# Seven-product feed-forward blocks: row sums on VectorE, kept gate blocks, gate products first, another order of banks

## The chip, the cores and the metric

The kernel runs on one NeuronCore of a Trainium2 chip. The metric is the device time of one execution in microseconds (us). Engines are named as in the profile: PE is TensorE (PEld its weight loads), DVE is VectorE, ACT is ScalarE, POOL is GpSimd, and SP is SyncE, which here does nothing but issue DMAs.

## The reference

The program is a two-layer streaming encoder on 256 rows of 1024 channels, all in float32:

```
h += 0.5 * ffn(rmsnorm(h)); h += mixer(rmsnorm(h)); h += 0.5 * ffn(rmsnorm(h))     # per layer
ffn(x) = (silu(x @ w1) * (x @ w3)) @ w2        # 1024 -> 2816 -> 1024
```

The mixer of layer 0 is a convolution module, that of layer 1 is latent attention, and a last rmsnorm ends it. So there are four feed-forward blocks (FFNs), counted 0 to 3 here as in the code. Their weights are most of what is read from HBM and their products most of the work on PE.

## The kernel before, in words

**Split weights and rows.** A float32 product is made of three passes of a faster matmul type: every weight block and every row block is kept as a high part and a low part. `mm3` (L325) issues the three matmuls high x low, high x high and low x high. A weight block is 128 x 2048 floats, 1 MB. `load` (L215 to L245) fetches it with one DMA on SP's queue into one of four `raw` buffers. Then, in two halves of 1024 columns, ACT casts the high part (L241) and DVE subtracts it from the block to get the low part (L242); `hi` and `lo` have five buffers each. The DMAs of a block are issued when one of the four raw buffers has been read for the last time.

**An FFN.** `ffn_in` (L807) runs the up products in chunks `c` = 0 to 5 of 512 gate columns (256 in the last). Chunk by chunk, two row tiles `tb` and two matrices (m = 0 for w1, m = 1 for w3) fill four PSUM banks `u[m, tb]`. ACT then takes the silu of `u[0, tb]` (L914), DVE multiplies it with `u[1, tb]` (L915), and `turn` (L810) brings the gate block into transposed form: DVE transposes 32 x 32 blocks (L445), four DMAs write the tile to DRAM, one reads it back in another order into the tile `gb` (L449, L453), and ACT and DVE split it into `Gh` and `Gl` (L816, L817). The down product (class `Rows`, L719) then sums over the 22 gate blocks into four banks `o[tb, d]`.

**Seven products in place of eight.** In FFNs 1, 2 and 3, chunk 3 of the up product and the first eight gate blocks of the down product are computed as a 2 x 2 block product with seven block products (`seven_products`, L348). One block product is 12 matmuls. The seven need sums and differences of blocks on both sides:

- of the weights: `load_seven` (L190 to L211) makes them on DVE in the raw buffers with four subtractions of 128 x 2048, at L201 and L202 (before the second block), L204 (before the third) and L206 (before the seventh). The high and low parts of all seven come at L210;
- of the rows: `forms_of` (L333) adds high and low parts on POOL (L339), makes four sums or differences of 128 x 512 on POOL (L343), and ACT and DVE split each (L344, L345). It works in the tile `rows4`. For the up product it is called ahead of chunk 2, for the down product after chunk 5. The split sums lie in gate columns that are not in use yet, or in the place of the FFN's own rows X once those have been read.

Between the products, results are copied or added from bank to bank, by the queue of each engine in order: after product 1, ACT copies bank `c11` to `c21`; after product 2, ACT copies `c22` to SBUF (`kept`); after product 3, DVE makes `c12 = c21 + kept`; after product 5, DVE makes `c22 = c21 + kept` (all L253 in the profile, since they are called through `urgent`). Product 2 is the first to write bank `c22`. Product 5 writes `c21` again, so it waits for the addition after product 3.

**What sets the order.** The code is traced in program order, and a planner decides at build time in which order each engine's instructions stand, from due order and an own timeline. `urgent` (L247) gives the instructions traced in it a higher priority, and remembers the last of them on each engine. `behind` (L182) adds to an instruction an edge that keeps it after the last six remembered ones of its engine; `load` calls it for the casts and low parts of ordinary blocks (L244), `load_seven` does not. `weights` (L266) hands out the next block, and `load_ahead` traces loads three blocks beyond it. So when the seven products begin, the loads of their blocks 0 to 2 have been traced ahead of the gate products (L915) of the chunk before, and blocks 3, 4, 5 and 6 are traced in products 1, 2, 3 and 4.

**Banks.** `bank("A", ...)` hands out four PSUM banks in turn; a new tile can be written when the last reader of the one before in its bank is done. The banks of the seven products were those of the chunk before, whose last readers are the gate products of L915.

Of the kernel before, what the change touches and what calls it, by code (L numbers as in the profile page):

```python
# [11 lines left out]
F32 = mybir.dt.float32  # L12
F32R = mybir.dt.float32r
# [27 lines left out]
W_BUFS = 5  # L41
# [48 lines left out]
def trunk(ctx: ExitStack, tc: tile.TileContext, x, xt, first, pos, invf, gfin, wdw,  # L90
          f1w13, f1w2, f2w13, f2w2, cw1, cw2, wa, wuq, wukv, wo, wpair, out):
    nc = tc.nc
# [12 lines left out]
    def uid(s):  # L105
        n_uid[0] += 1
        return f"{s}_{n_uid[0]}"
# [4 lines left out]
    def bank(tag, name):  # L112
        return ps.tile([P, 512], F32, tag=tag, name=uid(name), bufs=BANKS[tag])
# [75 lines left out]
    def load_seven(j, four, b, pieces):  # L189
        hi = wp.tile([P, HB], F32R, tag="hi", name=uid("hi"))  # L190
        lo = wp.tile([P, HB], F32R, tag="lo", name=uid("lo"))
        n = len(loaded)
        if j == 0:
            b[11], b[12] = fetched(four[0]), fetched(four[1])
        elif j == 1:
            b[22] = fetched(four[3])
        elif j == 2:
            b[21] = fetched(four[2])
        sub = nc.vector.tensor_sub
        if j == 1:  # L200
            sub(b[11], b[12], b[11])  # L201
            sub(b[12], b[22], b[12])  # L202
        elif j == 2:
            sub(b[11], b[22], b[11])  # L204
        elif j == 6:
            sub(b[11], b[21], b[11])  # L206
        raw = b[(11, 11, 11, 21, 12, 22, 11)[j]]
        for i in range(pieces):
            c = slice(i * HB // pieces, (i + 1) * HB // pieces)
            casts[n, i] = nc.scalar.copy(hi[:, c], raw[:, c]), sub(lo[:, c], raw[:, c], hi[:, c].bitcast(F32))  # L210
        return hi, lo  # L211

    def load(src, pieces=1):
# [46 lines left out]
    def load_ahead(ahead=W_BUFS - 2):  # L260
        load_to(min(len(blocks), n_used[0] + ahead))
# [5 lines left out]
    def weights(n=1, more=True):  # L267
        out = []
        for _ in range(n):
            n_used[0] += 1  # L270
            if more:
                load_ahead()
            else:
                load_ahead(0)
            out.append(loaded[n_used[0] - 1])
        return out
# [53 lines left out]
        nc.tensor.matmul(o, ah, bh, start=False, stop=False, skip_group_check=seeded)  # L330
        return nc.tensor.matmul(o, al, bh, start=False, stop=stop, skip_group_check=seeded)  # L331

    def forms_of(xh, xl, sh, sl):  # L333


        sh, sl = (z.rearrange("p k t -> p (k t)").rearrange("p (n k t) -> p n k t", n=4, t=P) for z in (sh, sl))
        x = rows4.rearrange("p n t -> p (n t)").rearrange("p (k t) -> p k t", t=S)
        add = nc.gpsimd.tensor_tensor
        add(x, xh.bitcast(F32), xl.bitcast(F32), op=ALU.add)  # L339
        x11, x12, x21, x22 = (x[:, 4 * a:4 * a + 4, tbs(tb)] for tb in range(2) for a in range(2))  # L340
        for n, out, left, right, op in ((0, x22, x21, x22, ALU.add), (2, x21, x11, x21, ALU.subtract),
                                        (1, x11, x22, x11, ALU.subtract), (3, x12, x12, x11, ALU.subtract)):
            add(out, left, right, op=op)  # L343
            nc.scalar.copy(sh[:, n], out)  # L344
            nc.vector.tensor_sub(sl[:, n], out, sh[:, n].bitcast(F32))  # L345
        return [(sh[:, n], sl[:, n]) for n in range(4)]
# [35 lines left out]
    def tbs(tb):  # L382
        return slice(tb * P, (tb + 1) * P)
# [53 lines left out]
                order(low, a.ins)  # L437
        return high

    def turn_blocks(pool, src, n, tag, after=()):  # L440
# [11 lines left out]
        b = pool.tile([P, 512], F32, tag=tag + "b", name=uid(tag + "b"), bufs=2)  # L452
        last_read[0] = nc.sync.dma_start(b[:, :w], d)  # L453
        return b[:, :w].rearrange("p (i t q) -> p t i q", i=4, q=32)

    class Norm:


        def __init__(self, gname, half=False, turn_by_dma=None):
            self.col = GCOL[gname]  # L460
            self.half = half

            self.pool = turn_by_dma
            self.turning = []
# [12 lines left out]
            self.turned = ()  # L477
            self.lows, self.highs = [], []

            self.between = None  # L480
# [236 lines left out]


    class Rows:  # L719
        def __init__(self, zh, zl, nk, last=False):  # L720
            self.zh, self.zl, self.nk, self.last = zh, zl, nk, last
            self.o = {(tb, d): bank("A", "o") for tb in range(NT) for d in range(2)}
            self.seeded = False

        def seven(self, forms):
            self.seeded = True
# [80 lines left out]
    def ffn_in(act, X, make_next, beside, apart, seven_up, seven_down):  # L807
        Gh = act.tile([P, NF, S], F32R, tag="Gh", name=uid("Gh"))
        Gl = act.tile([P, NF, S], F32R, tag="Gl", name=uid("Gl"))
        def turn(c, tb, w, g):  # L810

            n = w // P
            f = slice(4 * c, 4 * c + n)
            bv = turn_blocks(act, g[:, :w], n, "g")
            gh = Gh[:, f, tbs(tb)].rearrange("p t (i q) -> p t i q", q=32)
            nc.scalar.copy(gh, bv)  # L816
            nc.vector.tensor_sub(Gl[:, f, tbs(tb)].rearrange("p t (i q) -> p t i q", q=32), bv, gh.bitcast(F32))  # L817
# [30 lines left out]
        for c in range(6):  # L848

            both = c == 5  # L850
# [61 lines left out]
            for tb in range(NT):  # L912
                s = tmp.tile([P, 512], F32, tag="s", name=uid("s"))
                nc.scalar.activation(s[:, :w], u[0, tb][:, :w], AF.Silu, scale=X.r[tb])  # L914
                nc.vector.tensor_mul(s[:, :w], s[:, :w], u[0, tb][:, w:] if both else u[1, tb])  # L915
                turn(c, tb, w, s)
        o = Rows(Gh, Gl, NF, make_next is Final)
# [849 lines left out]
```

## Time and profile before

| | |
|---|---|
| median of 3 runs | 961.84 us (960.57 to 962.07) |
| the profiled execution: its own time | 960.39 us |
| its span, first to last instruction | 958.4 us |
| mean granted TensorE clock | 0.977 |
| PE busy | 902.6 us (94%), 4233 matmuls |
| DVE busy | 750.2 us (78%) |
| ACT busy | 546.6 us (57%) |
| POOL busy | 215.0 us (22%) |
| HBM | 207 GB/s over the span |

FFN 1 runs from about 278 us of the span, FFN 2 from about 470 us and FFN 3 from about 759 us. Rows of the profile name a line, an engine, an operation, the tiles written and read (out<-in), a shape and a count; then come busy time and the mean ns of one, or start and duration. In square brackets or at the end stands the idle time of the engine just ahead and what ended it. In the view by windows the columns are, for each stretch, the busy time and the count of PE, PEld, DVE, ACT and POOL, then the granted TensorE clock, the DMA engines' busy share and GB/s. `x2` behind a DVE row of L210 or L242 means two halves of a block.

### The profile page before, as it was taken

The numbers are of one execution on the slowest core, as the hardware profiler recorded it, in microseconds if no ns is written. First come the engines' busy times: TensorE is split into PE (matmuls) and PEld (weight loads), VectorE is DVE, ScalarE is ACT, GpSimd is POOL, SyncE is SP. The second block draws the span as 40 slices with busy tenths as digits, with TensorE's granted clock in tenths as the row PEclk, the third lists the DMA queues.
The fourth block names the chain that finished last, engine by engine and source line by source line (L and its number), as shares of the span: only waits on it lengthen the run. The fifth ranks groups of instructions, "written<-read, shape, count | busy, mean of one in ns | idle before, by whom it ended". The sixth has DMA issues, their size and how long they took to land.

```text
span 958.4 us, 12212 instructions
## 1 busy us (share of the span) xinstructions
PE 902.6 (94%) x4233; PEld 754.3 (79%) x4233; DVE 750.2 (78%) x1036; ACT 546.6 (57%) x917; POOL 215.0 (22%) x289
## 2 busy tenths in 40 slices
PE   9999999999999969989999499799999999599797
PEld 7888888898988858868888388688998888378686
DVE  5896654499988899895697989965866698988953
ACT  7655443598966346474463553753866663463742
POOL 1720000199925060000150600002300150600000
PEclk9999999999999989999999889999999999899999
DMA  9987775344138809578568086685635367095631
GB/s 332 361 318 264 244 245 198 132 176 151 70 84 317 297 20 364 179 249 301 160 218 283 9 311 224 195 312 155 220 122 207 124 234 279 3 343 192 207 156 44
DMA packets 71054, 198.94 MB, mean 208 GB/s; under 512 B 12368, under 2 KB 41936, under 8 KB 51664
## 3 DMA queue, kind: packets, MB, share of 16 engines
q1 hardware_dynamic: 70560, 197.47, 58.7%
q10 hardware_dynamic: 432, 0.69, 0.2%
q8 instruction: 33, 0.54, 0.2%
q14 instruction: 29, 0.24, 0.1%
HBM read 181.87 MB, written 16.25 MB: 207 GB/s over the span
## 4 chain that ended last, share of the span: by engine, by line
PE 46%; DVE 27%; DMA 14%; issue 7%; ACT 3%; SPq 2%; DVEq 0%; ACTq 0%
PE o L327 8%; PE o L331 8%; PE o L330 8%; DVE lo L210 7%; DVE lo L242 6%; DMA gb<-gd 4%; DMA raw<-in_f2w 4%; PE u L330 3%; PE u L327 3%; PE u L331 3%; DMA gd<-gt 3%; DVE acc L1045 2%; DVE raw L204 2%; PE u L956 2%; PE gate L956 2%
## 5 line engine op out<-in xcount | busy, mean ns | idle before, releaser
L242 DVE TENSOR_TENSOR lo<-raw,hi 128x1024 fp32r<-128x1024 f32 (+1 forms) x244 | 309.1, 1309 | 77.8 <-ACT hi L241 77.4
L241 ACT CAST hi<-raw 128x1024 fp32r<-128x1024 f32 (+1 forms) x246 | 244.2, 1044 | 130.0 <-PE o L331 54.3
L327 PE MATMUL u<-lo,Xh 128*128 128x512 f32 x612 | 238.4, 389 | 0.1
L330 PE MATMUL u<-hi,Xh 128*128 128x512 f32 x612 | 238.1, 389 | 0.0
L331 PE MATMUL u<-hi,Xl 128*128 128x512 f32 x612 | 237.7, 389 | 0.0
L327 PEld LDWEIGHTS u<-lo,Xh 128*128 128x128 f32 x612 | 114.9, 188 | 24.5 <-ACT Xh L564 0.7
L331 PEld LDWEIGHTS u<-hi,Xl 128*128 128x128 f32 x612 | 114.9, 188 | 24.4 <-DVE Xl L432 0.5
L330 PEld LDWEIGHTS u<-hi,Xh 128*128 128x128 f32 x612 | 114.9, 188 | 23.7
L404 POOL TENSOR_TENSOR ms<-ss 128x1 f32<-128x1 f32 x16 | 8.8, 554 | 470.5 <-ACT junk L396 470.5
L330 PE MATMUL o<-hi,Gh 128*128 128x512 f32 (+1 forms) x296 | 114.3, 386 | 0.0
L331 PE MATMUL o<-hi,Gl 128*128 128x512 f32 (+1 forms) x296 | 114.1, 386 | 0.0
L327 PE MATMUL o<-lo,Gh 128*128 128x512 f32 (+1 forms) x296 | 114.1, 386 | 0.0
L210 DVE TENSOR_TENSOR lo<-raw,hi 128x1024 fp32r<-128x1024 f32 x84 | 108.9, 1331 | 5.8 <-ACT hi L210 5.8
L210 ACT CAST hi<-raw 128x1024 fp32r<-128x1024 f32 x84 | 83.1, 1046 | 51.0 <-DVE raw L204 41.2
L816 ACT CAST Gh<-gb 128x512 fp32r<-128x512 f32 (+1 forms) x48 | 27.9, 582 | 78.0 <-DMA gb<-gd 78.0
L331 PEld LDWEIGHTS o<-hi,Gl 128*128 128x128 f32 x296 | 55.6, 188 | 11.3
L330 PEld LDWEIGHTS o<-hi,Gh 128*128 128x128 f32 x296 | 55.6, 188 | 11.2
L327 PEld LDWEIGHTS o<-lo,Gh 128*128 128x128 f32 x296 | 55.6, 188 | 11.2
L817 DVE TENSOR_TENSOR Gl<-gb,Gh 128x512 fp32r<-128x512 f32 (+1 forms) x48 | 30.8, 643 | 35.7 <-ACT Gh L816 35.6
L343 POOL TENSOR_TENSOR rows<-rows 128x512 f32<-128x512 f32 x24 | 55.0, 2290 | 1.9
L327 PE MATMUL u<-lo,Gh 128*128 128x512 f32 x48 | 22.1, 461 | 34.5 <-DVE s L915 20.7
L1045 DVE SCALAR_TENSOR_TENSOR acc<-V,dw,acc 128x128 f32<-128x128 f32 (+1 forms) x174 | 53.9, 390 | 0.0
(256 smaller groups left out, 1336.2 us busy)
## 6 DMA issues: line engine op xcount, KB each, us to landing
raw<-in_f2w SPq DMA_DIRECT2D x66, 1024.0 KB, 6.2
raw<-in_f1w SPq DMA_DIRECT2D x62, 1024.0 KB, 6.1
raw<-in_cw SPq DMA_DIRECT2D x12, 1024.0 KB, 4.8
gd<-gt SPq DMA_DIRECT2D x160, 64.0 KB, 3.3
gb<-gd SPq DMA_DIRECT2D x40, 256.0 KB, 5.0
raw<-in_wo SPq DMA_DIRECT2D x4, 1024.0 KB, 4.8
hd<-rows SPq DMA_DIRECT2D x56, 64.0 KB, 2.4
rows<-hd SPq DMA_DIRECT2D x14, 256.0 KB, 2.8
```

Of the source, the lines that this page charges most:

```text
L204: sub(b[11], b[22], b[11])
L210: casts[n, i] = nc.scalar.copy(hi[:, c], raw[:, c]), sub(lo[:, c], raw[:, c], hi[:, c].bitcast(F32))
L241: casts[len(loaded), i] = (nc.scalar.copy(hi[:, c], raw[:, c]), low.tensor_sub(lo[:, c], raw[:, c], hi[:, c].bitcast(F32)))
L242: low.tensor_sub(lo[:, c], raw[:, c], hi[:, c].bitcast(F32)))
L327: mm = nc.tensor.matmul(o, ah, bl, start=start, stop=False, skip_group_check=seeded)
L330: nc.tensor.matmul(o, ah, bh, start=False, stop=False, skip_group_check=seeded)
L331: return nc.tensor.matmul(o, al, bh, start=False, stop=stop, skip_group_check=seeded)
L343: add(out, left, right, op=op)
L816: nc.scalar.copy(gh, bv)
L817: nc.vector.tensor_sub(Gl[:, f, tbs(tb)].rearrange("p t (i q) -> p t i q", q=32), bv, gh.bitcast(F32))
L956: mm = nc.tensor.matmul(u[:, t], w[:, c], X.x[:, k, t], start=(k == 0), stop=(k == KT - 1))
L1045: dve_last.append(nc.vector.scalar_tensor_tensor(out if j == j1 - 1 else y, v, w, y, op0=ALU.mult, op1=ALU.add))
```

## The change

1. **Row sums.** `forms_of` is cut in two. `sums_of_rows` makes the four sums on DVE in place. `forms_of` splits them on ACT and DVE as before. For the up product the sum of high and low parts (128 x 2048) is made on DVE too, into a buffer of the `raw` pool, and the call stands one chunk earlier, ahead of chunk 1. For the down product there is no sum of high and low parts any more: the gate blocks of chunks 0 and 1 are read back from DRAM into `rows4` instead of `gb`, stay there, and the four sums are made from them.
2. **Gate products.** L915 is `urgent` in the chunk before a seven-product chunk and in that chunk itself (chunks 2 and 3), not in chunk 5.
3. **Order of weight work.** In `load_seven`, every subtraction on DVE and every cast on ACT is put `behind` the urgent ones.
4. **Banks.** The four banks are asked for in the order c11, c21, c22, c12. `load_ahead(W_BUFS - 1)` ahead of `weights(1, False)` loads up to the same block as `weights()` did.

```diff
 # load_seven
-        sub = nc.vector.tensor_sub
+        def sub(out, left, right):
+            ins = nc.vector.tensor_sub(out, left, right)
+            behind(ins)
+            return ins
...
             casts[n, i] = nc.scalar.copy(hi[:, c], raw[:, c]), sub(lo[:, c], raw[:, c], hi[:, c].bitcast(F32))
+            behind(casts[n, i][0])
 # forms_of
-        add = nc.gpsimd.tensor_tensor
-        add(x, xh.bitcast(F32), xl.bitcast(F32), op=ALU.add)
...
+    def sums_of_rows(x11, x12, x21, x22):
+        sums = [(0, x22, x21, x22, ALU.add), (2, x21, x11, x21, ALU.subtract), (1, x11, x22, x11, ALU.subtract),
+                (3, x12, x12, x11, ALU.subtract)]
+        for n, out, left, right, op in sums:
+            nc.vector.tensor_tensor(out, left, right, op=op)
+        return [(n, out) for n, out, *_ in sums]
 # product, in seven_products
-            (hi, lo), = weights()
+            load_ahead(W_BUFS - 1)
+            (hi, lo), = weights(1, False)
 # Rows.__init__
-            self.o = {(tb, d): bank("A", "o") for tb in range(NT) for d in range(2)}
+            self.o = {key: bank("A", "o") for key in (((0, 0), (1, 0), (1, 1), (0, 1)) if seeded else
+                                                      ((0, 0), (0, 1), (1, 0), (1, 1)))}
 # turn, in ffn_in
-            bv = turn_blocks(act, g[:, :w], n, "g")
+            bv = turn_blocks(act, g[:, :w], n, "g", (), rows4[:, 2 * c + tb, :] if seven_down and c < 2 else None)
 # the chunks, in ffn_in
-            if seven_up and c == min(seven_up) - 1:
-                forms = forms_of(X.xh, X.xl, Gh[:, 14:], Gl[:, 14:])
+            if seven_up and c == min(seven_up) - 2:
+                xs = rawp.tile([P, HB], F32, tag="raw", name=uid("xs")).rearrange("p (k t) -> p k t", t=S)
+                nc.vector.tensor_add(xs, X.xh.bitcast(F32), X.xl.bitcast(F32))
+                sums = sums_of_rows(*(xs[:, 4 * a:4 * a + 4, tbs(tb)] for tb in range(2) for a in range(2)))
+                forms = forms_of(sums, Gh[:, 14:], Gl[:, 14:])
...
-                for key in ((0, 0), (0, 1), (1, 0), (1, 1)):
+                for key in ((0, 0), (0, 1), (1, 1), (1, 0)):
...
-                nc.vector.tensor_mul(s[:, :w], s[:, :w], u[0, tb][:, w:] if both else u[1, tb])
+                mul = urgent(nc.vector.tensor_mul) if c in seven_up or c + 1 in seven_up else nc.vector.tensor_mul
+                mul(s[:, :w], s[:, :w], u[0, tb][:, w:] if both else u[1, tb])
...
-            sums = (xp.tile([P, KT, S], F32R, tag=tag, name=uid("rows")) for tag in ("Xh", "Xl"))
-            o.seven(forms_of(Gh[:, :8], Gl[:, :8], *sums))
+            z11, z21, z12, z22 = (rows4[:, n, :] for n in range(4))
+            both = (xp.tile([P, KT, S], F32R, tag=tag, name=uid("rows")) for tag in ("Xh", "Xl"))
+            o.seven(forms_of(sums_of_rows(z11, z12, z21, z22), *both))
```

More of the change, by code (lines that the diff above doesn't have):

```diff
@@ L331, in mm3, with forms_of @@
         return nc.tensor.matmul(o, al, bh, start=False, stop=stop, skip_group_check=seeded)
-    def forms_of(xh, xl, sh, sl):
-        sh, sl = (z.rearrange("p k t -> p (k t)").rearrange("p (n k t) -> p n k t", n=4, t=P) for z in (sh, sl))
-        x = rows4.rearrange("p n t -> p (n t)").rearrange("p (k t) -> p k t", t=S)
-        add = nc.gpsimd.tensor_tensor
[L339 to L346, printed above, removed]
+    def sums_of_rows(x11, x12, x21, x22):
[4 more added lines that the diff above has]
+        return [(n, out) for n, out, *_ in sums]
+    def forms_of(sums, sh, sl):
+        sh, sl = (z.rearrange("p k t -> p (k t)").rearrange("p (n c) -> p n c", n=4) for z in (sh, sl))
+        out = {}
+        for n, x in sums:
+            if len(x.shape) == 2:
+                high, low = (z[:, n].rearrange("p (t i q) -> p t i q", t=4, q=32) for z in (sh, sl))
+                x = x.rearrange("p (i t q) -> p t i q", i=4, q=32)
+            else:
+                high, low = (z[:, n].rearrange("p (k t) -> p k t", t=P) for z in (sh, sl))
+            nc.scalar.copy(high, x)
+            nc.vector.tensor_sub(low, x, high.bitcast(F32))
+            out[n] = [z[:, n].rearrange("p (k t) -> p k t", t=P) for z in (sh, sl)]
+        return out
     def seven_products(xh, xl, forms, banks):
@@ L438, in split_rows, with turn_blocks @@
         return high
-    def turn_blocks(pool, src, n, tag, after=()):
+    def turn_blocks(pool, src, n, tag, after=(), b=None):
         w = n * P
@@ L451, in turn_blocks @@
                 order(dma, a.ins)
-        b = pool.tile([P, 512], F32, tag=tag + "b", name=uid(tag + "b"), bufs=2)
+        if b is None:
+            b = pool.tile([P, 512], F32, tag=tag + "b", name=uid(tag + "b"), bufs=2)
         last_read[0] = nc.sync.dma_start(b[:, :w], d)
@@ L719, in trunk, with __init__ @@
     class Rows:
-        def __init__(self, zh, zl, nk, last=False):
+        def __init__(self, zh, zl, nk, last=False, seeded=False):
             self.zh, self.zl, self.nk, self.last = zh, zl, nk, last
-            self.o = {(tb, d): bank("A", "o") for tb in range(NT) for d in range(2)}
-            self.seeded = False
+            self.o = {key: bank("A", "o") for key in (((0, 0), (1, 0), (1, 1), (0, 1)) if seeded else
+                                                      ((0, 0), (0, 1), (1, 0), (1, 1)))}
+            self.seeded = seeded
         def seven(self, forms):
-            self.seeded = True
             seven_products(self.zh, self.zl, forms, self.o)
@@ L914, in ffn_in @@
                 nc.scalar.activation(s[:, :w], u[0, tb][:, :w], AF.Silu, scale=X.r[tb])
[L915 removed]
+                mul = urgent(nc.vector.tensor_mul) if c in seven_up or c + 1 in seven_up else nc.vector.tensor_mul
+                mul(s[:, :w], s[:, :w], u[0, tb][:, w:] if both else u[1, tb])
                 turn(c, tb, w, s)
[L917 removed]
+        o = Rows(Gh, Gl, NF, make_next is Final, seven_down)
         if seven_down:
[L919 to L920 removed]
+            z11, z21, z12, z22 = (rows4[:, n, :] for n in range(4))
+            both = (xp.tile([P, KT, S], F32R, tag=tag, name=uid("rows")) for tag in ("Xh", "Xl"))
+            o.seven(forms_of(sums_of_rows(z11, z12, z21, z22), *both))
         for i in range(4 if seven_down else 0, NF // 2 - (3 if apart else 2)):
```

## The prediction

> **What bounds the kernel now.** I read the list of waits of PE first, since the page has PE busy for 94% of the span: what can be won lies in the other 6% and in the clock.
>
> ```profile
> PE u L327 <- DVE s L915: 20.7, 2, 11.9
> PE u L327 <- issue: 13.3, 1, 13.3
> PE o L327 <- DVE s L915: 8.4, 3, 3.9
> PE o L327 <- DVE o L253: 5.5, 3, 2.8
> ```
>
> Columns: us in total, times, longest. Nine waits make 47.9 us, and all stand inside the six seven-product stages: three ahead of product 2 of an up stage (u; one in each of FFNs 1, 2, 3), three ahead of product 2 of a down stage (o, 8.4), three ahead of product 5 of a down stage (o, 5.5). The rest of PE's idle time is under 2 us in all. The second row names "issue"; the timelines of FFN 2 tell who it is. First PE (with the last matmuls of product 1 in FFNs 1 and 3 around it), then DVE and POOL in the same stretch:
>
> ```profile
> 345.93 0.39 PE L330 MATMUL u<-hi,Xh 128*128 128x512 f32 x1
> 346.16 0.39 PE L331 MATMUL u<-hi,Xl 128*128 128x512 f32 x1
> ...
> 537.66 0.39 PE L331 MATMUL u<-hi,Xl 128*128 128x512 f32 x1
> 551.31 0.76 PE L327 MATMUL u<-lo,Gh 128*128 128x512 f32 x1 [13.26 <-issue]
> ...
> 823.90 0.39 PE L331 MATMUL u<-hi,Xl 128*128 128x512 f32 x1
> ```
>
> ```profile
> 533.96 6.57 DVE L204 TENSOR_TENSOR raw<-raw,raw 128x2048 f32<-128x2048 f32 x1
> 541.70 5.65 DVE L210 TENSOR_TENSOR lo<-raw,hi 128x1024 fp32r<-128x1024 f32 x3 [1.17 <-ACT hi L210]
> 547.26 3.35 DVE L206 TENSOR_TENSOR raw<-raw,raw 128x2048 f32<-128x2048 f32 x1
> 550.54 0.67 DVE L915 TENSOR_TENSOR s<-s,u 128x512 f32<-128x512 f32 x1
> ```
>
> ```profile
> 532.96 5.42 POOL L339 TENSOR_TENSOR rows<-Gh,Gl 128x2048 f32<-128x2048 f32 x1 [38.76 <-DVE Gl L817]
> ```
>
> See three things. PE resumes at 551.31, right behind the first gate product L915 (550.54 + 0.67 = 551.21): product 2 wants the bank that L915 reads. That gate product belongs to chunk 2, which PE left before product 1, but it stands on DVE's queue behind weight work, even behind L206, which serves product 7. And L204 took 6.57 us beside POOL's L339, which POOL began as soon as the last gate block was split, in the middle of DVE's rush. What an instruction of that size takes alone is the last row here (groups by line; mean ns behind the comma):
>
> ```profile
> L210 ACT CAST hi<-raw 128x1024 fp32r<-128x1024 f32 x84 | 83.1, 1046 | 51.0 <-DVE raw L204 41.2 <-DVE raw L201 5.4 <-issue 3.1
> ...
> L817 DVE TENSOR_TENSOR Gl<-gb,Gh 128x512 fp32r<-128x512 f32 x40 | 27.4, 687 | 31.3 <-ACT Gh L816 31.3
> ...
> L201 DVE TENSOR_TENSOR raw<-raw,raw 128x2048 f32<-128x2048 f32 x6 | 13.8, 2292 | 0.2
> ```
>
> Last, the clock behind such waits, by windows (PE first, the granted clock third from the end):
>
> ```profile
> 355.30:361.40 6.10, 6.06 (x14) 4.79 (x15) 6.10 (x7) 0.54 (x2) 0.52 (x1) 0.50 0.55 173
> 412.70:416.10 3.40, 3.40 (x9) 2.72 (x9) 3.40 (x6) 2.59 (x4) 0.00 (x0) 0.50 0.69 272
> 551.30:555.90 4.60, 4.59 (x11) 3.63 (x12) 4.60 (x6) 0.00 (x0) 0.00 (x0) 0.50 0.57 171
> 836.20:839.30 3.10, 3.07 (x7) 2.48 (x8) 3.10 (x4) 0.00 (x0) 0.00 (x0) 0.50 0.25 48
> 894.20:897.40 3.20, 3.11 (x8) 2.51 (x9) 3.20 (x6) 3.13 (x5) 0.00 (x0) 0.51 0.92 328
> ```
>
> At full clock a matmul starts every 0.23 us (345.93, 346.16). 14, 9, 11, 7 and 8 matmuls should take 11.3 us where 20.4 went: 9.1 us lost. Waits and slow clock together are **57.0 us**, the most that a change of these stages can return.
>
> **The change, part by part.**
>
> *Sums on DVE.* Removed are all L343 and L339 of POOL. Added per FFN: up, one 128x2048 addition (2.29, as L201) and four of 128x512 (0.69, as L817): 5.05 us; down 4 x 0.69 = 2.76 us. Together 3 x 7.8 = 23.4 us on DVE. What DVE gets back is the collision. In the up stage of FFN 2 above: L204 6.57 - 2.29 = 4.3; L206 3.35 - 2.29 = 1.1; three halves of L210 5.65 - 3.45 (the row at 419.40 below) = 2.2; in all 7.5 us. In chunk 0 of the same FFN, beside POOL's up sums, the chain of waits has
>
> ```profile
> 486.29 10.14 DVE lo L242 x5
> ```
>
> where 5 x 1.15 = 5.8 would do: 4.4 us more. So about 12 us return per FFN for 7.8 spent. The up sums land where 4.4 us leave and 5.05 come: I take 0 there, between -1 and +5 us an FFN. The cover is that PE has no wait in chunks 1 and 2, with blocks prepared ahead.
>
> The Trainium skill, "Perfetto Trace Analysis", Optimizing Scalar/DVE Operations, says that a saturated DVE may be worth relieving even with GPSIMD, and adds that the two share an SBUF read port, so that it might not help. By its first half this change goes the wrong way (the third rival below); by its second half, and by the 6.57 us here, it does not.
>
> *The raw buffer* that the up sum borrows leaves three of four for its stay. SP's queue holds raw fetches, gate writes and gate reads in one order, so all of them stand behind a fetch that waits for a buffer. Three blocks are 3 x 24 matmuls = 16 us of PE; a buffer's round is a landing (6.2, the row below), two casts (2.1) and two halves (2.3), 11 us. I take nothing; 5 us an FFN if that cover fails.
>
> ```profile
> raw<-in_f2w SPq DMA_DIRECT2D x66, 1024.0 KB, 6.2
> ```
>
> *Gate products urgent, weight work behind them.* Blocks 0 to 2 are traced ahead of L915 in program order, so L204 and their halves may stay ahead; block 3's halves and L206 come behind by the new edge. Wait ahead of product 2, up: in FFN 2, L204 ends at 533.96 + 2.29 = 536.25, the casts at 538.3, the last half at 539.5, L915 at 540.2. PE is free at 537.9: wait 2.3 us. In FFN 1 and FFN 3 the same sum starts from
>
> ```profile
> 342.60 8.82 DVE L210 TENSOR_TENSOR lo<-raw,hi 128x1024 fp32r<-128x1024 f32 x3 [1.18 <-ACT hi L210]
> ...
> 818.90 6.58 DVE L204 TENSOR_TENSOR raw<-raw,raw 128x2048 f32<-128x2048 f32 x1
> ```
>
> 342.60 + 2.3 + 0.7 = 345.6 against PE free at 346.4: 0. 818.90 + 2.29 + 2.1 + 1.2 + 0.7 = 825.2 against 824.1: 1.1. Sum 3.4. But the four down sums become ready just here (POOL's row: it began behind L817), and DVE's plan has room exactly where block 3 is held back. With 2.76 us ahead of L915 the waits are 2.0, 5.1 and 3.9. Bounds 3.4 and 11.0; the nearest row, POOL's start at 532.96, has them here: **11.0**.
>
> *Behind product 2, up.* DVE must do, before product 7: blocks 3 to 6 (8 x 1.15), L206 2.29, the second gate product 0.7, two transposes and two L817 2.8 (each as L817), two additions 1.4, and wait 1.05 for a cast behind L206: 17.4 us. PE needs 60 x 0.23 = 13.8. Late by 3.6 at most; without transposes and L817, for which no product waits, by 0.8. I take 1.5 a stage: **4.5** (0 to 10.8).
>
> *Down.* The order ahead of product 2 and of product 5, in FFN 1:
>
> ```profile
> 407.70 2.29 DVE L206 TENSOR_TENSOR raw<-raw,raw 128x2048 f32<-128x2048 f32 x1
> 409.90 1.22 DVE L210 TENSOR_TENSOR lo<-raw,hi 128x1024 fp32r<-128x1024 f32 x1
> 411.03 0.69 DVE L817 TENSOR_TENSOR Gl<-gb,Gh 128x512 fp32r<-128x512 f32 x1
> 411.64 0.41 DVE L915 TENSOR_TENSOR s<-s,u 128x256 f32<-128x256 f32 x1
> ...
> 419.40 3.45 DVE L210 TENSOR_TENSOR lo<-raw,hi 128x1024 fp32r<-128x1024 f32 x3
> 422.77 0.69 DVE L253 TENSOR_TENSOR o<-o,p 128x512 f32<-128x512 f32 x1
> ```
>
> L915 of chunk 5 is not urgent, but L206 now stands behind the urgent addition after product 3 and so behind L915: 2.29 us less ahead of product 2. Of 8.4 (longest 3.9) remain 3.9 - 2.29 = **1.6**. The addition L253 loses block 6's two halves (2.3 us) ahead of it: of 5.5 (longest 2.8) remain **0.5**. New is the end: from product 1 to product 7 DVE has L206 2.29, seven halves 8.05, gate products 0.8, four low parts 2.76, two additions 1.4, a cast's wait 1.05, together 16.4, and 3 us of transposes and L817; PE needs 72 x 0.23 = 16.6. Between 0 and 2.8 a stage; 1 each: **3.0** (0 to 8.4). ACT's casts of blocks 4 to 6 now stand behind the copies after products 1 and 2, with two products (5.5 us) or more for 2.1 + 2.3 us of work: nothing.
>
> *Banks and load_ahead.* PE resumed behind the first gate product, so product 2 has the earlier bank already, and the loads reach the same block: 0, at best a gate product (0.7 us) a stage.
>
> *Clock.* Of the gaps left, two (5.1 and 3.9 us) are as long as ones that cost 1.4 to 1.5 us: **3.0** (0 to 7).
>
> Left: 11.0 + 4.5 + 1.6 + 0.5 + 3.0 + 3.0 = 23.6 us of 57.0, so 33.4 us are won. The profiled execution took 960.39 us (span 958.4 and 2.0 around it), 1.45 below the median of 961.84. 960.39 - 33.4 = 927.0, as a median **928.4 us**. By the bounds alone 908 to 945.
>
> A check from the other side, by windows of FFN 2:
>
> ```profile
> 500.00:535.00 35.00, 35.00 (x156) 28.96 (x156) 27.97 (x28) 12.31 (x16) 2.04 (x1) 1.00 0.64 217
> 535.00:580.00 45.00, 31.74 (x131) 25.76 (x130) 40.70 (x34) 24.73 (x28) 13.15 (x5) 0.85 0.58 208
> ```
>
> The DVE column, less 7.5 us of collision, has 33.2 us in the up stage where PE has some 30 at full clock. 7 us of DVE lie free just before it, but only four blocks' worth can be prepared ahead. With 2.76 us of sums on top DVE has 6 us more than PE: some wait must remain in each FFN, and a forecast of none would be too good.
>
> **The rivals.**
>
> *The order stays.* If the plan keeps L915 behind block 3 and L206, only the collisions go. FFN 2: 539.5 + 1.2 + 2.3 + 0.7 = 543.7, wait 5.8; FFN 1 2.6; FFN 3 4.5; the down sums ahead add 8.3; the down waits stay at 13.9, the clock near 7: 42 of 57 stay, **947 us**. For it: the plan put L206 ahead of a gate product traced before it. Against: the new edges forbid just that.
>
> *All covered.* The down sums find DVE's 7 free us, and nothing is late behind product 2: 3.4 + 1.6 + 0.5 stay, **910 us**. Against: the check above.
>
> *DVE becomes the bound (slower).* Place: the stretch from L204 to product 2. If DVE there is full whatever the order, PE's waits stay as they are and 3 x 2.76 us of sums come on top: **970 us**. It decides if L204 and its neighbours, without POOL beside them, give back less than the 7.8 us an FFN that are added; the row of 6.57 us speaks for 12. This is also what the skill's first half would give.
>
> *The change does not do what it says* (bank order, load_ahead): costed at 0 in the forecast already.
>
> **How the numbers follow.** Forecast (915 to 941) 0.52; order stays (941 to 952) 0.21; all covered (905 to 915) 0.15; no change 0.03; DVE-bound 0.09. The range 906 to 950 leaves out the last two and the tails of the second and third, together under 0.2. About 0.2% (1.9 us) is what a measurement of this kernel can tell from no change: faster 0.88, same 0.03, slower 0.09.
>
> **What would show it.** Right: no POOL rows at L339 and L343; L204 at 2.3 us in all stages; L915 of chunk 2 on DVE ahead of L206; PE's waits for L915 and L253 under 20 us, with new small ones for `lo` at products 6 and 7. Wrong: L206 still ahead of L915; DVE idle ahead of an urgent instruction while halves wait behind it; PE waiting in chunks 1 or 2 for `lo` (sums or raw buffer), or longer rows of half clock.

## The result, and the profile after

The changed kernel takes 907.91 us (median of 4 runs, 907.25 to 912.39) against 961.21 us for the kernel before on the same chip: a ratio of 0.9458, 95% interval 0.9424 to 0.9492. The forecast was 928.4 us with a range of 906 to 950. So the sign and the range held, and the size did not: 53 us were won where 33 were forecast, close to the rival "all covered" (910 us). The time lies 1.9 us above the lower end of the range and just below the 908 us that the sum's own bounds allow. The profiled execution took 907.97 us with a span of 906.2.

The waits of PE of the changed kernel (us in total, times, longest), and from its page the clock and the groups of weight work. Line numbers have moved: L332, L335, L336 are the three matmuls of `mm3`, L200 is the subtraction in `load_seven` (the four weight subtractions, raw<-raw,raw, and the low parts, lo<-raw,hi, alike), L247 the low parts of ordinary blocks, L934 or L258 the gate products, L357 the low parts of the row sums, and L258 also the copies and additions between banks. Other kernels below have the same lines a few numbers away:

```profile
PE o L336 <- DVE rows L357: 3.6, 3, 1.2
PE o L332 <- DVE o L258: 2.4, 3, 0.8
PE u L332 <- DVE u L258: 1.1, 1, 1.1
```

```profile
PE 891.5 (98%) x4233; PEld 747.3 (82%) x4233; DVE 727.6 (80%) x1063; ACT 547.0 (60%) x917; POOL 128.4 (14%) x259
...
PEclk9999999999999999999999999999999999999999
...
L247 DVE TENSOR_TENSOR lo<-raw,hi 128x1024 fp32r<-128x1024 f32 (+1 forms) x244 | 287.5, 1218 | 67.2 <-ACT hi L246 66.4
...
L200 DVE TENSOR_TENSOR lo<-raw,hi 128x1024 fp32r<-128x1024 f32 x84 | 98.9, 1213 | 5.0 <-ACT hi L214 5.0
...
L200 DVE TENSOR_TENSOR raw<-raw,raw 128x2048 f32<-128x2048 f32 x24 | 54.8, 2281 | 0.3
```

Of 47.9 us of waits in the seven-product stages 7.1 are left, and the granted clock is at 90% or more in all 40 slices of the span (mean 0.998 against 0.977). DVE is busy for 727.6 us against 750.2, although it makes 27 instructions more: the halves that took 1309 and 1331 ns in the mean now take 1218 and 1213.

The up stage of FFN 2, first PE, then DVE (L344 is the row sums, L832 the low part of a gate block):

```profile
522.33 0.39 PE L336 MATMUL u<-hi,Xl 128*128 128x512 f32 x1
522.55 0.39 PE L332 MATMUL u<-lo,Gh 128*128 128x512 f32 x1
```

```profile
503.14 4.62 DVE L200 TENSOR_TENSOR raw<-raw,raw 128x2048 f32<-128x2048 f32 x2
507.68 2.35 DVE L200 TENSOR_TENSOR lo<-raw,hi 128x1024 fp32r<-128x1024 f32 x2
509.95 1.29 DVE L832 TENSOR_TENSOR Gl<-rows,Gh 128x512 fp32r<-128x512 f32 x2
511.15 2.28 DVE L200 TENSOR_TENSOR raw<-raw,raw 128x2048 f32<-128x2048 f32 x1
513.35 1.41 DVE L344 TENSOR_TENSOR rows<-rows 128x512 f32<-128x512 f32 x2
...
518.16 0.68 DVE L258 TENSOR_TENSOR s<-s,u 128x512 f32<-128x512 f32 x1
...
520.03 0.69 DVE L258 TENSOR_TENSOR s<-s,u 128x512 f32<-128x512 f32 x1 [0.45 <-PE u L336]
```

Product 2 starts at 522.55, 0.22 us after the last matmul of product 1 started: no wait. Both gate products are done before that, and the second one waits for PE, not PE for it. The down sums do stand ahead of the gate products, as forecast, and cost nothing. The first row shows why: the first weight subtraction starts 522.55 - 503.14 = 19.4 us ahead of the end of product 1. In the kernel before it started at

```profile
522.86 2.29 DVE L201 TENSOR_TENSOR raw<-raw,raw 128x2048 f32<-128x2048 f32 x1
528.16 0.69 DVE L817 TENSOR_TENSOR Gl<-gb,Gh 128x512 fp32r<-128x512 f32 x1 [3.01 <-ACT Gh L816]
528.77 2.28 DVE L202 TENSOR_TENSOR raw<-raw,raw 128x2048 f32<-128x2048 f32 x1
```

against 537.9 for the end of product 1, 15.0 us ahead, and then waited 3.01 us for a gate block from DRAM. L204, the third subtraction, stood 3.9 us ahead of the end of product 1 and now stands 11.4 ahead: 4.4 us of this are the earlier start, the other 3.1 mostly the wait for the gate block, which is gone. The forecast had taken the start of L204 as given. How far DVE is ahead of PE at the first weight subtraction of the up stage is called the **lead** below. In FFNs 1, 2 and 3 it was 15.3, 15.0 and 15.4 us, and is 20.6, 19.4 and 19.4.

### The profile page after: what moved, and what is told of

Same layout as the page of the kernel before. It is cut to its first block, busy times and chain, and to the rows that moved or that the text cites. A ratio compares the mean times of both kernels' runs of the same rounds, so it can differ in the third digit from the quotient of the medians.

```text
span 906.2 us, 12201 instructions
## 1 busy us (share of the span) xinstructions
PE 891.5 (98%) x4233; PEld 747.3 (82%) x4233; DVE 727.6 (80%) x1063; ACT 547.0 (60%) x917; POOL 128.4 (14%) x259
## 4 chain that ended last, share of the span: by engine, by line
PE 69%; DVE 16%; DMA 8%; issue 3%; ACT 3%; SPq 1%; DVEq 0%; ACTq 0%
PE u L332 9%; PE u L336 9%; PE u L335 9%; PE o L336 9%; PE o L332 9%; PE o L335 9%; DVE lo L200 3%; DVE acc L1065 3%; DVE lo L247 2%; DMA raw<-in_f2w 2%; PE u L976 2%; PE gate L976 2%; PE u L392 2%; DVE raw L200 2%; DMA gd<-gt 1%
## 5 line engine op out<-in xcount | busy, mean ns | idle before, releaser
L247 DVE TENSOR_TENSOR lo<-raw,hi 128x1024 fp32r<-128x1024 f32 (+1 forms) x244 | 287.5, 1218 | 67.2 <-ACT hi L246 66.4
L332 PE MATMUL u<-lo,Xh 128*128 128x512 f32 x612 | 238.3, 389 | 0.2 <-ACT Xh L579 0.2
L336 PE MATMUL u<-hi,Xl 128*128 128x512 f32 x612 | 238.2, 389 | 0.0
L335 PE MATMUL u<-hi,Xh 128*128 128x512 f32 x612 | 238.1, 389 | 0.0
L332 PEld LDWEIGHTS u<-lo,Xh 128*128 128x128 f32 x612 | 114.9, 188 | 24.3 <-ACT Xh L579 0.6
L336 PEld LDWEIGHTS u<-hi,Xl 128*128 128x128 f32 x612 | 114.9, 188 | 24.2 <-DVE Xl L446 0.5
L335 PEld LDWEIGHTS u<-hi,Xh 128*128 128x128 f32 x612 | 114.9, 188 | 23.9
L332 PE MATMUL o<-lo,Gh 128*128 128x512 f32 (+1 forms) x296 | 114.3, 387 | 0.0
L335 PE MATMUL o<-hi,Gh 128*128 128x512 f32 (+1 forms) x296 | 114.3, 386 | 0.0
L336 PE MATMUL o<-hi,Gl 128*128 128x512 f32 (+1 forms) x296 | 114.3, 386 | 0.0
L200 DVE TENSOR_TENSOR lo<-raw,hi 128x1024 fp32r<-128x1024 f32 x84 | 98.9, 1213 | 5.0 <-ACT hi L214 5.0
L332 PEld LDWEIGHTS o<-lo,Gh 128*128 128x128 f32 x296 | 55.6, 188 | 11.6 <-DVE lo L200 0.3
L335 PEld LDWEIGHTS o<-hi,Gh 128*128 128x128 f32 x296 | 55.6, 188 | 11.3
L336 PEld LDWEIGHTS o<-hi,Gl 128*128 128x128 f32 x296 | 55.6, 188 | 11.1
L200 DVE TENSOR_TENSOR raw<-raw,raw 128x2048 f32<-128x2048 f32 x24 | 54.8, 2281 | 0.3
L831 ACT CAST Gh<-gb 128x512 fp32r<-128x512 f32 (+1 forms) x36 | 20.5, 571 | 55.1 <-DMA gb<-gd 55.0
L1086 ACT ACTIVATE prod<-V,dw 128x128 f32<-128x128 f32 (+1 forms) x128 | 45.8, 415 | 2.0 <-POOL Y L1087 1.0
L778 DVE SCALAR_TENSOR_TENSOR h<-o,rh,h 128x512 f32<-128x512 f32 (+1 forms) x18 | 12.9, 719 | 31.4 <-PE o L336 31.4
```

The costliest lines, as they stand in the source:

```text
L200: ins = nc.vector.tensor_sub(out, left, right)
L247: low.tensor_sub(lo[:, c], raw[:, c], hi[:, c].bitcast(F32)))
L332: mm = nc.tensor.matmul(o, ah, bl, start=start, stop=False, skip_group_check=seeded)
L1086: prods_last.append(nc.scalar.activation(p, v, AF.Copy, scale=w))
```

## The experiments

Two theories were set against each other first. A: POOL's collisions with DVE cost the time. B: the order of DVE's queue cost it.

| kernel | sums | urgent gate products, edges | median us | ratio to before, 95% interval |
|---|---|---|---|---|
| before | POOL | no | 961.2 | |
| e2_order_only | POOL | yes | 939.93 | 0.9779 (0.9732 to 0.9825) |
| e3_sums_only | DVE, gate blocks kept | no | 928.67 | 0.9662 (0.9629 to 0.9695) |
| e1_pool_sums | POOL, gate blocks kept | yes | 930.84 | 0.9692 (0.9661 to 0.9723) |
| changed kernel | DVE, gate blocks kept | yes | 907.91 | 0.9458 (0.9424 to 0.9492) |

**e1_pool_sums**

```diff
-            nc.vector.tensor_tensor(out, left, right, op=op)
+            nc.gpsimd.tensor_tensor(out, left, right, op=op)
-                nc.vector.tensor_add(xs, X.xh.bitcast(F32), X.xl.bitcast(F32))
+                nc.gpsimd.tensor_tensor(xs, X.xh.bitcast(F32), X.xl.bitcast(F32), op=ALU.add)
```

> The changed kernel with one thing undone: the sums of rows (the 128x2048 addition and the four of 128x512 of each up stage, the four of each down stage) are made on POOL again; urgent gate products, weight work behind them and kept gate blocks stay. Theory A (the collision of POOL's sums with DVE's weight work is what cost the time): some DVE rows of weight work at about twice their time again, PE waits of 3 to 8 us for a gate product ahead of product 2 of the up stages, some half clock, 920 to 935 us. Theory B (DVE's order is what cost the time): within 4 us of the changed kernel, 906 to 912 us.

930.84 us: theory A's figure. PE's waits in the up stages are back:

```profile
PE u L332 <- DVE u L258: 8.0, 3, 3.4
PE u L332 <- DVE s L258: 6.0, 3, 3.1
```

The lead is 14.8, 14.8 and 13.6 us in the three FFNs. But the weight subtractions themselves take 2.29 us each in this run: most of what is late was late before them (in FFN 2 the two halves behind the third subtraction take 3.45 us, 1.1 too much). Since the gate blocks are kept, there is no 128x2048 addition on POOL beside L204 here.

**e2_order_only** (the kernel before with the `urgent` gate products and the `behind` edges of the diff above)

> The kernel before with only the order changed: gate products urgent in chunks 2 and 3, seven-product weight work behind the urgent instructions. Sums stay on POOL, with the addition of high and low parts for the down product and the old place of the call. Theory A (collisions): most of the up waits stay, since L204 and the halves behind it still run beside POOL's 5.4 us addition: waits of 5 to 8 us per up stage, 925 to 945 us. Theory B (order): up waits under 3 us each, down waits as in the changed kernel, 908 to 920 us.

939.93 us, inside A's range. PE still waits 18.1 us for gate products ahead of product 2 of the up stages (the row "issue" is FFN 2's, as in the prediction):

```profile
PE u L332 <- DVE s L258: 10.0, 2, 6.6
PE u L332 <- issue: 8.1, 1, 8.1
PE u L332 <- DVE u L258: 4.9, 3, 2.5
PE o L336 <- DVE rows L350: 3.4, 3, 1.2
```

The down waits, 13.9 us before, are as short as in the changed kernel (3.4, and 2.4 for the additions). The up waits fall from 34.5 us to 23.0. So the order alone takes 8.1 us of waits from the down stages and 11.5 from the up stages, and 21.3 us from the time.

e1 and e2 together show one thing more. Their leads are nearly the same (e2: 15.2, 15.4 and 15.0 us), but e1 waits 6.0 us for gate products in the up stages, and e2 18.1. In e2 the addition of 128x2048 of the down sums still stands on POOL, and in FFN 2 the third weight subtraction runs beside it:

```profile
527.19 6.56 DVE L200 TENSOR_TENSOR raw<-raw,raw 128x2048 f32<-128x2048 f32 x1
```

So the collision beside L204 does cost something when the lead is short: e1 is 9.1 us faster than e2. The two kernels also differ in the place of the call for the up sums and in the buffers of the gate blocks, so not all of this need be the collision.

**e3_sums_only** (the changed kernel without `urgent` gate products, without both `behind` calls, and with the old order of banks; the gate products are L929 here, the additions between banks L255)

> The changed kernel with only the sums: made on DVE, with kept gate blocks and the earlier call, but no urgent gate products, no edges on the weight work and the old order of banks. Theory A (collisions): the up waits go (under 3 us each), the down waits stay near the 13.9 us of before, 918 to 930 us. Theory B (order): gate products still wait behind the weight work of product 7, waits of 4 to 6 us per up stage and 13.9 us down, 940 to 950 us (the forecast's rival of an order that stays had 947).

928.67 us, inside A's range and far from B's. PE no longer waits ahead of product 2 of the up stages, and the down waits stay as they were:

```profile
PE o L329 <- DVE s L929: 8.9, 3, 4.3
PE u L329 <- DVE u L255: 5.2, 3, 1.9
PE o L329 <- DVE o L255: 4.5, 3, 2.8
```

The sums alone give 32.5 us, the order alone 21.3, both together 53.3: the times add. The waits do not. The sums alone take 29.3 us from the up waits (34.5 to 5.2) and 0.5 from the down waits, the order alone 11.5 and 8.1, both together 33.4 and 7.9. The part of the order is then the down stages and what is left of the up stages. That the times add so well is not explained; the mean granted clock (0.977 before, 0.988 and 0.987 with one part, 0.998 with both) says that some slow stretches go only with both. Neither theory is right by itself.

"Sums only" is also not quite free of order. Without edges or priority the planner put the first gate product ahead of the fourth weight subtraction (L206 before) by itself, in all three FFNs. These are rows of FFN 2:

```profile
526.68 0.68 DVE L929 TENSOR_TENSOR s<-s,u 128x512 f32<-128x512 f32 x1
...
528.42 2.29 DVE L200 TENSOR_TENSOR raw<-raw,raw 128x2048 f32<-128x2048 f32 x1
```

What a collision costs with DVE's order held fixed is measured by e9 below.

**e4_no_urgent**

```diff
-                mul = urgent(nc.vector.tensor_mul) if c in seven_up or c + 1 in seven_up else nc.vector.tensor_mul
-                mul(s[:, :w], s[:, :w], u[0, tb][:, w:] if both else u[1, tb])
+                nc.vector.tensor_mul(s[:, :w], s[:, :w], u[0, tb][:, w:] if both else u[1, tb])
```

> The changed kernel without the higher priority of the gate products; the edges that keep seven-product weight work behind the urgent copies and additions stay. Theory A: no loss, since DVE reaches the gate products before PE needs them, 906 to 911 us. Theory B: the gate product slips behind one or two halves of weight work, a wait of 1 to 3 us in each up stage, 911 to 918 us.

916.12 us (914.82 to 922.07), inside B's range, but not for B's reason. The gate products still end ahead of product 2. What PE waits for is the low part of the last block, ahead of product 7:

```profile
PE u L332 <- DVE lo L200: 5.4, 3, 2.9
```

The subtraction for this block is not late: it starts 7.4 us behind the end of product 1 in FFN 2, and 7.8 in the changed kernel. Late are ACT's casts of the block, which stand on ACT's queue behind the cast of a gate block, and this one waits for its DMA:

```profile
536.67 0.62 ACT L831 CAST Gh<-gb 128x512 fp32r<-128x512 f32 x1 [3.34 <-DMA gb<-gd]
537.19 1.99 ACT L214 CAST hi<-raw 128x1024 fp32r<-128x1024 f32 x2
```

In FFNs 1 and 3 the same cast waits 2.38 and 4.46 us. In the changed kernel both gate blocks are cast earlier, and the casts of the last block wait only for the subtraction:

```profile
532.72 2.00 ACT L214 CAST hi<-raw 128x1024 fp32r<-128x1024 f32 x2 [1.12 <-DVE raw L200]
```

The gate products end 0.6 to 1.8 us later against PE than in the changed kernel, and the casts of their blocks start 3 to 6 us later; what lies between was not followed. That the priority is worth some 8 us is measured; that it is by this wait alone is not, since it makes 5.4.

The next four ask which sums matter. P is the forecast's account (the down sums beside L204 are what costs; the up sums are an even trade), Q says that the up sums make the lead.

**e5_down_pool** (only the four down sums on `nc.gpsimd`)

> The changed kernel with only the four down sums of each FFN on POOL again (beside the weight work of the up stage); the up sums stay on DVE. Theory P (the forecast's account: the time lies in the collision beside L204, and the up sums were an even trade): the weight work of the up stage is slowed by 3 to 5 us per FFN and waits for the gate product return, 916 to 930 us. Theory Q (what counts is that DVE reaches the first weight subtraction of the stage 5 us earlier, and this comes from the up sums): the first subtraction still starts 19 us or more ahead of the end of product 1, the collision is covered by that lead, 907 to 913 us.

908.72 us (907.08 to 910.34): no loss to be told from the changed kernel's runs, and inside Q's range. The lead is 20.6, 19.4 and 19.3 us. A collision is there, first on POOL, then on DVE:

```profile
511.42 9.29 POOL L344 TENSOR_TENSOR rows<-rows 128x512 f32<-128x512 f32 x4 [48.18 <-DVE Gl L832]
```

```profile
514.71 3.48 DVE L200 TENSOR_TENSOR lo<-raw,hi 128x1024 fp32r<-128x1024 f32 x2 [1.18 <-ACT hi L214]
518.11 0.67 DVE L258 TENSOR_TENSOR s<-s,u 128x512 f32<-128x512 f32 x1
```

Two halves take 3.48 us in place of 2.35, and the gate product still starts at 518.11, as in the changed kernel (518.16). But this collision is small. The halves lose 1.1 us, and DVE is rid of 2.76 us of sums; the 128x2048 addition, which stood beside L204 before, is not in this kernel. So the run shows that the place of the four small sums does not matter. It does not show that the lead would cover the 6.57 us of the kernel before; no run has both that addition on POOL and the long lead.

**e6_up_pool** (the up sums on `nc.gpsimd`)

> The changed kernel with only the four up sums of 128x512 of each FFN on POOL again (in chunks 0 and 1); their 128x2048 addition and the down sums stay on DVE. Theory P: an even trade, 906 to 911 us. Theory Q: the first weight subtraction of the up stage starts some 15 us ahead of the end of product 1 again in place of 19 to 20, gate products behind product 1, waits of 2 to 5 us per up stage, 916 to 932 us.

The kernel that ran had the 128x2048 addition of the up sums on POOL too, unlike what this text says, so it moves all up sums. 931.98 us (0.9701, 0.9677 to 0.9725): all that e1 lost comes from the up sums. Lead 15.6, 14.6 and 13.8 us. That the up sums are an even trade, P's second half, is refuted.

**e9_pool_beside.** The planner orders DVE differently with the sums on POOL, so e6 does not tell a collision from another order. This kernel does: the instructions of DVE and ACT stand in the same order as in the changed kernel, and POOL gets additions whose output nothing reads, behind the up sums.

```diff
+                junk = act.tile([P, 512], F32, tag="pj", name=uid("pj"))
+                for q in range(8):
+                    nc.gpsimd.tensor_tensor(junk.rearrange("p (k t) -> p k t", t=S), X.xh[:, 2 * (q % 4):2 * (q % 4) + 2].bitcast(F32),
+                                            X.xl[:, 2 * (q % 4):2 * (q % 4) + 2].bitcast(F32), op=ALU.add)
```

> The changed kernel with idle work added on POOL and nothing else: behind the up sums of each FFN, eight additions of 128x512 from the rows X into a tile that nothing reads (about 17 us of POOL, where POOL's up sums took 13 us before). DVE's instructions stand in the same order as in the changed kernel. If POOL's reading beside DVE is what made DVE late: halves of weight work at 2.3 us in place of 1.2 in chunks 0 and 1, the first weight subtraction of the up stage some 5 to 8 us later against PE, waits for gate products again, 922 to 940 us. If it was the other order that the planner chose with the sums on POOL: 906 to 911 us.

931.60 us (930.75 to 932.49): 23.7 us lost to work whose result nobody uses. In chunk 0 of FFN 2, POOL first, then DVE of the same run (L878 is the idle work, L873 the addition of high and low parts, L344 a row sum):

```profile
474.99 12.14 POOL L878 TENSOR_TENSOR pj<-Xh,Xl 128x512 f32<-128x512 f32 x5 [0.29 <-DVE Xl L580]
```

```profile
475.91 3.38 DVE L873 TENSOR_TENSOR xs<-Xh,Xl 128x2048 f32<-128x2048 f32 x1
479.21 6.77 DVE L247 TENSOR_TENSOR lo<-raw,hi 128x1024 fp32r<-128x1024 f32 x3
485.91 1.77 DVE L344 TENSOR_TENSOR xs<-xs 128x512 f32<-128x512 f32 x1
```

And the same three in the changed kernel:

```profile
467.14 2.29 DVE L873 TENSOR_TENSOR xs<-Xh,Xl 128x2048 f32<-128x2048 f32 x1
469.34 3.49 DVE L247 TENSOR_TENSOR lo<-raw,hi 128x1024 fp32r<-128x1024 f32 x3
472.75 0.68 DVE L344 TENSOR_TENSOR xs<-xs 128x512 f32<-128x512 f32 x1
```

11.9 us against 6.5. Shortly before them, four instructions that make the low parts of the rows X take 3.67 us in place of 1.23, so DVE has lost 7.9 us in all. 40 us later the lead is 12.1 us (517.63 to 529.7) in place of 19.4, and PE waits:

```profile
529.47 0.39 PE L336 MATMUL u<-hi,Xl 128*128 128x512 f32 x1
533.42 0.77 PE L332 MATMUL u<-lo,Gh 128*128 128x512 f32 x1 [3.56 <-issue]
```

```profile
517.63 4.62 DVE L200 TENSOR_TENSOR raw<-raw,raw 128x2048 f32<-128x2048 f32 x2
```

Of the 7.9 us, 7.3 are still missing there. DVE does have idle time on the way, but it cannot use it: its queue stands still for a gate block on its way through DRAM, with the next transposition behind it (1.31 us for the same instruction in the changed kernel):

```profile
512.72 0.69 DVE L832 TENSOR_TENSOR Gl<-rows,Gh 128x512 fp32r<-128x512 f32 x1 [3.61 <-ACT Gh L831]
```

The collision is shown as the cause of the lost lead.

**e8_not_kept** (the gate blocks go to `gb` as before, and DVE adds `Gh` and `Gl`, 128x2048, ahead of the down sums)

> The changed kernel without kept gate blocks: the gate blocks are read back into gb as before, and DVE adds their high and low parts (one more 128x2048 addition per FFN) ahead of the four down sums. By durations 2.29 us more of DVE in the up stage. If DVE has the slack that its lead in the changed kernel suggests (gate products end 2 to 4 us ahead of the end of product 1): up to 1 us per FFN, 907 to 911 us. If DVE is the bound of the stage: 2.3 us and more per FFN, 914 to 922 us.

911.06 us, but its runs spread from 909.24 to 919.13 (interval 0.9449 to 0.9541), and they overlap with those of the changed kernel. The median lies at the upper end of the estimate with slack and below the range of the bound. With the sums on DVE, whether the kept blocks are worth 0 or 3 us stays open.

**The order of the banks** has no run of its own. With the old order, the program that is built has the same instructions in the same order with the same waits on all five engines, and differs in the names of banks alone.

**e7_forms_urgent.** What is left in the changed kernel are the waits for L357 and the additions in the down stages.

```diff
-            o.seven(forms_of(sums_of_rows(z11, z12, z21, z22), *both))
+            o.seven(urgent(forms_of)(sums_of_rows(z11, z12, z21, z22), *both))
```

> The changed kernel with the split of the four down sums (high and low parts) made urgent, so that their four low parts stand two halves of weight work earlier on DVE. If the 3.6 us that PE still waits for low parts in product 2 of the down stages is an order on DVE: these waits go, 903 to 906 us. If the low parts are late because ACT's high parts or the rows X are late: no change, 907 to 909 us. If the two halves moved behind them are needed at once: a new wait of up to 2 us per FFN ahead of product 3 or 4, 907 to 912 us.

904.44 us (903.66 to 904.65; 0.9408, 0.9386 to 0.9431). All four runs are below all four of the changed kernel, though the intervals of the two ratios just touch. The waits for the low parts are gone, those for the additions with them:

```profile
PE u L332 <- DVE u L258: 1.3, 1, 1.3
...
PE o L332 <- DVE lo L200: 0.5, 2, 0.3
PE o L332 <- ACT o L258: 0.4, 1, 0.4
```

**e10_late_load** (e7, and in product 3 `load_ahead` is called behind the addition)

> The kernel with urgent low parts of the down sums (e7) and one step more: in product 3 the load of weight block 5 is traced behind the urgent addition after that product, so that its halves stand behind the addition on DVE. If the 0.8 us per FFN ahead of product 5 of the down stages (and the 1.1 us up) is only that order: these waits go, 901 to 903.5 us. If block 5 or the subtraction for block 6 then comes late for products 6 and 7: new waits there of 1 us or more per stage, 904 to 908 us.

905.17 us (901.95 to 905.30), not to be told from e7. The up wait of 1.3 us goes, and the waits for `lo` and for a copy on ACT grow from 0.5 and 0.4 us to 0.9 and 1.1. Some 2 us of waits are left in either: little more is to be had from this order.

## Why the prediction was right in sign and range, and 20 us too high

By its own terms, forecast and measured waits (us over the three FFNs):

| term | forecast | measured |
|---|---|---|
| up, ahead of product 2 | 11.0 | 0 |
| up, behind product 2 | 4.5 | 1.1 |
| down, product 2 | 1.6 | 3.6 |
| down, product 5 | 0.5 | 2.4 |
| down, end | 3.0 | 0 |
| slow clock behind waits | 3.0 | 0 |
| sum of 57.0 that stays | 23.6 | 7.1 |

The 49.9 us that this accounts for are most of the 52.4 by which the profiled executions differ (960.39 and 907.97); 2.5 us were not assigned to a row.

- **What bounds the kernel** was right: nearly all of the 57 us could be won, and they lay in the six stages.
- **"Sums on DVE ... I take 0 there" is the step that failed.** The up sums were not an even trade. The price of POOL's up sums was read from one row of the chain of waits, 10.14 us for five halves, 4.4 too much. The timeline of DVE has the whole stretch:

```profile
481.15 15.27 DVE L242 TENSOR_TENSOR lo<-raw,hi 128x1024 fp32r<-128x1024 f32 x6 [0.59 <-ACT hi L241]
```

  Six halves should take 6.9 us: 8.4 too much, not 4.4. A row of a chain holds only what lies on the chain. Against 5.05 us of sums that leaves 3.3 us, and DVE was not idle from there until 508.6 us. DVE's total agrees: it got back 46.0 us (23.4 of sums and 22.6 less busy), 15.3 us an FFN, where the forecast had about 12.
- **The same step then failed a second time, in what it fed.** The wait of 11.0 us ahead of product 2 was worked out from L204's start in the trace of before, as if nothing earlier moved it. With the up sums on DVE the lead grew from 15.0 to 19.4 us in FFN 2, and L204 came 7.5 us earlier against PE. e6 and e9 show what it costs to lose the lead to POOL's up sums, or to idle work in their place: 24 us. The forecast's 7.5 us beside L204 were real too: at a lead of 15 us the kernel with that addition on POOL (e2) is 9.1 us slower than one without (e1). What they would cost at the long lead was not run.
- **Down sums ahead of the gate products**: the order was right, its price (7.6 us) was covered by the lead.
- **Weight work behind the gate products and the additions**: right. e3 keeps 13.4 us of down waits, the changed kernel 6.0. What is left is another wait than forecast: low parts behind four halves of weight work, in the rows of DVE in the down stage of FFN 2:

```profile
570.82 4.59 DVE L200 TENSOR_TENSOR lo<-raw,hi 128x1024 fp32r<-128x1024 f32 x4
575.33 2.49 DVE L357 TENSOR_TENSOR rows<-rows,rows 128x512 fp32r<-128x512 f32 x4
```

- **The check from the other side misled.** It found DVE 6 us over PE in the up stage and took that for waits that must remain. It saw 7 us of DVE free just before the stage and did not count them, since only four blocks can be prepared ahead. The changed kernel did use them: in the 35 us that end about 3 us ahead of the end of product 1 of FFN 2 DVE is busy for 31.1 us, against 28.0 in the same stretch before. This is the rival "all covered" (0.15), down sums in DVE's free time and next to nothing late behind product 2; the check had marked it down. The range held because it was drawn wide enough for that rival, not because the sum was right.
- **The rival of an unchanged order** had 947 us. e3 comes nearest and took 928.67. It is not that case in full, since the planner moved the first gate product ahead of L206 there, and with the lead of 20.6, 19.2 and 19.7 us PE did not wait for it. The slower rival, a full DVE, did not come: DVE gave 23.4 us and got more back (727.6 against 750.2 us).
- **Raw buffer, banks, load_ahead at 0**: nothing in the trace speaks against it; PE has no wait in chunks 1 and 2.
- **Clock at 3.0**: it measured 0, since no gap of the length that the forecast expected was left.
- **The signs that it named**: the rows of POOL are gone, the 24 weight subtractions take 2.24 to 2.29 us, the gate products of chunk 2 stand ahead of the fourth weight subtraction (L206 before), and PE waits 3.5 us for the additions and none for gate products. The new waits for `lo` at products 6 and 7 did not come.

## What to carry to other kernels

Work that is moved to an idle engine may slow a busy one far ahead of the place where PE waits: compare durations of the same instruction with and without the other engine beside it, over whole stretches of the timeline. Before taking a start time from the trace of before into a sum, ask whether the change moves what stands ahead of it; how far a helper is ahead of PE when a rush begins can matter as much as what happens in the rush. And two edits that look like one remedy can be worth separate sums. A table of both, one and none costs two runs, but where a planner sets the order, look at the order in each of them: a kernel without one edit may differ in more than that edit.

## What the runs showed of the hardware that was not expected

Beside a row of POOL additions, DVE's subtractions and additions with two inputs in SBUF got through about once per POOL addition: six halves took 15.27 us next to the five additions of POOL's up sums (6.9 us alone), and a 128x2048 addition 3.38 us in place of 2.29 in e9. POOL pays as well: of its eight 128x512 additions in FFN 2 of e9, the first three, beside which DVE had to wait, take 1.29 to 1.30 us each, and the five that stand among DVE's instructions 2.14 to 3.23. The third of them:

```profile
473.40 1.30 POOL L878 TENSOR_TENSOR pj<-Xh,Xl 128x512 f32<-128x512 f32 x1 [0.29 <-DVE Xl L580]
```

The Trainium skill, "SBUF — State Buffer", Who interferes with whom, says that a DVE instruction with two SBUF inputs contends with a GpSimd instruction that reads SBUF, since its second input comes through a shared read interface, and that such contention is an exclusive lock; these rows agree. In time, the eight additions of e9 cost DVE 7.9 us in FFN 2, and the kernel 23.7 us over three FFNs. This came through the waits of PE that followed, and through the slow clock around them, as in these windows of e9 (granted clock third from the end):

```profile
349.00:352.40 3.40, 3.40 (x10) 2.66 (x9) 3.40 (x5) 0.57 (x1) 0.00 (x0) 0.50 0.32 77
533.30:536.70 3.40, 3.28 (x8) 2.64 (x9) 3.37 (x5) 1.00 (x2) 0.00 (x0) 0.50 0.32 75
```

Waits of up to 1.2 us, all that the changed kernel has, were followed by no such window.
